# Instructions that consume a transfer, held behind the six traced ahead of them on their engine

## The chip, the cores and the metric

One core of a Trainium2 chip runs the whole program in one launch. The metric is the device time of that core in microseconds (us). Its engines, each with an instruction queue of its own, are TensorE (PE: matmuls and transposes), VectorE (DVE), ScalarE (ACT), GpSimd (POOL) and SyncE (SP, which only issues transfers). Transfers (DMA) run beside them.

## The reference, cut to what matters

One layer of a flow-matching backbone for two groups of tokens: 128 context tokens and 2048 sample tokens of width 1024. Tokens are normed and modulated, one projection makes the columns of three branches, and the branches are merged with sigmoid gates:

```python
proj = jnp.einsum('btd,de->bte', xn, w_in)
qkv, beta, dec, z_a, u_b, v_b, z_b, x_c, z_c, gates = jnp.split(proj, points, axis=-1)
...
o, s_f, s_b = delta_bidir(q, k, v, g, beta, s0_f, s0_b)     # A: chunked gated delta rule, both directions
o_a = rmsnorm(o, o_norm_g) * silu(z_a)
o_b = chunk_sgu(u_b, v_b, sgu_norm_g, w_spatial, b_spatial) * silu(z_b)   # B: gating over chunks of 128
o_c = fourier_mix(x_c, grid) * silu(z_c)                                  # C: Fourier mixing
pb = jnp.einsum('btnw,nwd->btnd', stack(o_a, o_b, o_c), w_branch)
merged = (sigmoid(gates) * pb).sum(over n)
out = jnp.einsum('btd,de->bte', merged, w_out)
```

In branch A each chunk solves a triangular system (which the kernel does with inverses of 32x32 blocks, the "base inverses", and two levels that join them), and a scan carries the state from chunk to chunk.

## The kernel before, in words

**Numbers.** Every float32 operand of a matmul is split into two float16 halves, hi and lo, and a product takes three matmuls (hi·hi, hi·lo, lo·hi; `mm3`, L161 is the line that all of them have). Before it is split an operand is scaled by a power of two that is found from its sum of squares.

**A weight's way** (`converting`, L194 to L223): a weight of 1024x128 (or 512x128 for a branch projection) is loaded into one of two staging buffers `wst` by SP (L204). ACT squares it and sums (L209, into `lo`, which is only scratch at that point: the rows read `wlo<-wst` or `blo<-wst`, each followed by a small read of the accumulator). DVE casts the sum (L175), PE multiplies it with a matrix of ones (`b<-wscb,ones16`), DVE makes the scale from the result (L183 to L187), ACT makes hi (L222, `whi` or `bhi`) and DVE lo (L223). `converting` is a generator, and `weight_step` takes one step of it at each tick of the main loops, so that the next weights are made while PE works with the present ones; `getw` takes the steps that are still missing when a weight is needed. `wnext` counts the weights that were asked for so far.

**The stages.** PE is given the tokens' projections first (branch A's inputs and its chunk matrices, then branch B, then branch C), then three merges, then the output projection. Branch A's scan (`scan`, 34 steps over both directions) runs between the other matmuls: a `Pace` object takes a step of its generator every so many microseconds of main work. A scan step reads `kn` and `v` of a chunk, splits them (`kn16`, L972; `v16`, L907, by `split`), multiplies with the state, joins the levels of the inverse (`level`, L847 to L895, with tiles `ES`, `N`, `Q`, `T`, `R`), and splits `u` and the state S (L907 again, since all of them call `split`). `finish` norms a chunk's output `o` (four squares at L1048 and four products at L1051 on ACT, a transpose on PE at L1055, a product on DVE at L1057 and a square at L1058 on ACT) and stores it.

**Base inverses** (`base_inverse`, five groups): two loads fill `XB`, DVE copies one half transposed (L788), then 31 steps of two DVE operations (L795, L796), two conversions (L801 on ACT, L802 on DVE), and a store to `ei` (L805), from which the levels load `ES` (L847).

**Branch C**: rows of the Fourier transform go through `X` (ACT L1284, DVE L1285 to L1287) between two sets of matmuls.

**Merges** (`merge`, branches 1, 2, 0): for each of eight column blocks `db`, a gate weight `gw` (1024x128) and a branch weight `bw` (512x128); for each of five token blocks 24 matmuls of 512 columns with `gw`, a sigmoid on ACT (L1385, `sg`), 12 matmuls with `bw` on the branch's output `big`, and a product on DVE. `big` is made from `obD` by `branch_block` (a load into one of three buffers `st`, the hi half on ACT at L1355, the lo half on DVE at L1356), for the first merge just ahead of its use, for the others in the last `db` of the merge before.

**Output** (`out_prep`): a row of `merged` is loaded, squared on ACT (L1460), split (L1462 for hi) and multiplied with the output weight `wohi`, `wolo`.

**What sets the order.** The code is traced in program order, and a list scheduler with a timeline model then places the instructions of each engine. It may lift an instruction past others that are traced ahead of it, if its data are ready by its model. Each engine runs its own list strictly in order: an instruction whose transfer has not landed holds back everything behind it.

## Time and profile before

| | |
|---|---|
| time, median of 3 runs | 2198.1 us (2195.02 to 2202.01) |
| the profiled execution's own time | 2200.3 us |
| its span | 2198.2 us |
| instructions | 42667 |
| mean transfer rate | 166 GB/s |
| 1700 to 2000 us: PE busy | 300.0 of 300 us |

The profile is of one execution. In a row in time order the columns are the start and the length in us, the engine, the line, the operation, `out<-in` with the names of the tiles, shapes and count, and in brackets the time that the engine stood idle before the row with what ended it. Matmul lengths overlap: 128x512 matmuls follow each other every 0.216 us though each is shown with 0.35 to 0.38 us. A row of `SPq` is the issue of a transfer. A group's row gives busy time, mean ns of one, and the idle time before its instructions by releaser.

### The profile page before, as it was taken

How to read it: one execution, taken by the hardware profiler on the slowest of the kernel's cores; microseconds unless marked ns; L12 is line 12 of the kernel's file. 1: busy time of each engine (PE TensorE's matmuls, PEld its weight loads, DVE VectorE, ACT ScalarE, POOL GpSimd, SP SyncE). 2: the span in 40 equal slices, each digit the busy share in tenths (PEclk: the TensorE clock that was granted, in tenths of full speed). 3: DMA queues.
4: the chain of work that ended last, by engine and by line, in shares of the span. 5: the costliest groups of instructions: out<-in, count | busy, mean ns of one | idle time of the engine just before them, and what ended most of it. 6: DMA issues, size and time to landing. Idle time of an engine off the chain costs nothing. (4 is left out here: it accounts for less than half of the span.)

```text
span 2198.2 us, 42667 instructions
## 1 busy us (share of the span) xinstructions
PE 2125.9 (97%) x16234; PEld 1213.1 (55%) x16234; DVE 1311.2 (60%) x3140; ACT 1014.4 (46%) x2345; POOL 707.5 (32%) x862
## 2 busy tenths in 40 slices
PE   7999999999999999899899999999999999999998
PEld 3565444455555587777555555555654444444443
DVE  5746745469979698466665555765674544223454
ACT  3644644345466474355544445655553422222332
POOL 1421433223333322432322223344532221222543
PEclk9999999999999999999999999999999999999999
DMA  8324733167777662444655556776664544324542
GB/s 280 141 87 149 260 117 110 61 203 231 241 229 239 198 192 83 126 130 137 203 172 162 164 164 185 240 212 209 200 198 151 168 125 133 118 78 123 174 148 103
DMA packets 304568, 365.09 MB, mean 166 GB/s; under 512 B 39426, under 2 KB 215787, under 8 KB 302315
## 3 DMA queue, kind: packets, MB, share of 16 engines
q1 hardware_dynamic: 289226, 302.19, 45.6%
q0 software_dynamic: 12688, 51.27, 6.4%
q10 hardware_dynamic: 2448, 8.91, 1.0%
q8 instruction: 127, 2.08, 0.4%
q14 instruction: 79, 0.64, 0.1%
HBM read 234.67 MB, written 127.62 MB: 165 GB/s over the span
## 5 line engine op out<-in xcount | busy, mean ns | idle before, releaser
L161 PE MATMUL b<-xh,whi 128*128 128x512 f16 (+1 forms) x1920 | 652.8, 349 | 0.4 <-DVE mrow L1391 0.4
L161 PE MATMUL b<-xl,whi 128*128 128x512 f16 (+1 forms) x1920 | 652.9, 348 | 0.0
L161 PE MATMUL b<-xh,wlo 128*128 128x512 f16 (+1 forms) x1920 | 651.9, 348 | 0.5 <-DVE wlo L223 0.5
L161 PEld LDWEIGHTS <-whi 128*128 128x128 f16 x3904 | 358.8, 98 | 330.0 <-issue 9.4
L161 PEld LDWEIGHTS <-wlo 128*128 128x128 f16 x1952 | 191.7, 98 | 180.8 <-issue 5.0
L161 PE MATMUL b<-big,bhi 128*128 128x512 f16 (+1 forms) x960 | 250.6, 347 | 2.4 <-ACT big L1355 1.9
L1395 POOL TENSOR_TENSOR mrow<-mrow,sg 128x512 f32<-128x512 f32 (+1 forms) x80 | 91.8, 1148 | 293.9 <-DVE sg L1394 225.7
L161 PE MATMUL b<-big,blo 128*128 128x512 f16 (+1 forms) x480 | 162.9, 347 | 0.0
L1385 ACT ACTIVATE sg<-b,winv 128x512 f32<-128x512 f32 (+1 forms) x120 | 74.1, 618 | 174.5 <-PE b L161 173.7
L644 POOL TENSOR_TENSOR cy<-cy,raw 128x545 f32<-128x545 f32 (+1 forms) x48 | 74.9, 1586 | 184.2 <-ACT raw L643 184.2
L161 PEld LDWEIGHTS <-xh 128*128 128x128 f16 x1496 | 117.0, 98 | 28.1
L1394 DVE SCALAR_TENSOR_TENSOR sg<-b,binv,sg 128x512 f32<-128x512 f32 (+1 forms) x80 | 53.4, 667 | 126.1 <-PE b L161 119.3
L161 PEld LDWEIGHTS <-bhi 128*128 128x128 f16 x960 | 86.5, 98 | 73.6 <-issue 2.1
L175 DVE CAST wscb<-wss 128x1 bf16<-128x1 f32 x93 | 14.3, 154 | 148.5 <-ACT wlo L209 67.3
L864 POOL COPY T<-ES 32x256 f16<-32x256 f16 x68 | 30.5, 449 | 202.3 <-DMA ES<-ei 167.1
L161 PE MATMUL b<-whi,xh 128*128 128x128 f16 x544 | 92.9, 219 | 0.0
L161 PE MATMUL b<-wlo,xh 128*128 128x128 f16 x544 | 92.9, 219 | 0.0
L161 PE MATMUL b<-whi,xl 128*128 128x128 f16 x544 | 92.9, 219 | 0.0
L161 PE MATMUL b<-wohi,mh 128*128 128x512 f16 x240 | 90.9, 379 | 1.4 <-ACT mh L1462 1.4
L161 PE MATMUL b<-wohi,ml 128*128 128x512 f16 x240 | 90.8, 379 | 0.3 <-DVE mscb L175 0.3
L161 PE MATMUL b<-wolo,mh 128*128 128x512 f16 x240 | 90.9, 379 | 0.0
L209 ACT ACTIVATE wlo<-wst 128x1024 f16<-128x1024 f32 x52 | 55.0, 1057 | 77.5 <-DMA wst<-in_w_in_dram 74.1
(456 smaller groups left out, 4285.4 us busy)
## 6 DMA issues: line engine op xcount, KB each, us to landing
wst<-in_w_in_dram SPq DMA_DIRECT2D x60, 512.0 KB, 4.9
qkv<-cy POOLq DMA_DIRECT2D x12, 1089.0 KB, 5.4
st<-br SPq DMA_DIRECT2D x48, 256.0 KB, 4.6
mrow<-mrg SPq DMA_DIRECT2D x18, 512.0 KB, 3.6
mrow<-mrg SPq DMA_DIRECT2D x16, 576.0 KB
mrg<-mrow POOLq DMA_DIRECT2D x16, 576.0 KB, 3.6
dc<-dec SPq DMA_DIRECT2D x17, 512.0 KB, 4.7
kq<-qkv SPq DMA_DIRECT2D x34, 256.0 KB, 4.6
```

The costliest lines, as they stand in the source:

```text
L161: PE.matmul(out, l, r, start=start, stop=stop)
L175: V.tensor_copy(sb16, ss)
L209: A.activation(w.lo, st, AF.Square, accum_out=ss)
L644: G.tensor_tensor(y[:, c0:c1], y[:, c0:c1], raw[:, 1 + c0:1 + c1], ALU.mult)
L864: G.tensor_copy(T16[rows(a0, b), :, :, b], ES[0:32, :, 2 * a0 + b, :, wT])
L1385: A.activation(sg, ps, AF.Sigmoid, scale=gw.inv)
L1394: V.scalar_tensor_tensor(sg, ps, binv[:, 1:2], sg, ALU.mult, ALU.mult)
L1395: G.tensor_tensor(mr, mr, sg, ALU.add)
```

## The change

A helper ties an instruction to the six that were traced just ahead of it on the same engine, with a dependency that carries no semaphore: the scheduler may no longer place it ahead of them, and nothing else waits. It is used at six places: the square of a weight, from the seventeenth weight asked for on; DVE's copy that begins a base inverse; the cast of `kn`; the split of `v` in the first step of each scan direction; ACT's half of a branch block; and the square of an output row.

```diff
+    def pinned(made, n=6):
+
+        ins = made.ins
+        before = (i for i in reversed(nc.cur_bb.bb.instructions) if i is not ins and i.engine == ins.engine)
+        for _, i in zip(range(n), before):
+            tc.add_manual_dep(ins, i.name, mybir.DependencyInfo(mybir.DependencyClass.NoSync, mybir.DependencyReason.DATA),
+                              reason="pinned")
+        return made
...
-        A.activation(w.lo, st, AF.Square, accum_out=ss)
+        sq = A.activation(w.lo, st, AF.Square, accum_out=ss)
+        if wnext[0] >= 16:
+            pinned(sq)
...
-        V.tensor_copy(b3(X[64:P, :]), tmp[64:P, :].rearrange("p (i j) -> p j i", j=32))
+        pinned(V.tensor_copy(b3(X[64:P, :]), tmp[64:P, :].rearrange("p (i j) -> p j i", j=32)))
...
-    def split(t_, src, scale=1.0):
-        A.activation(t_[:, 0, :], src, AF.Copy, scale=scale)
+    def split(t_, src, scale=1.0, pin=False):
+        hi = A.activation(t_[:, 0, :], src, AF.Copy, scale=scale)
+        if pin:
+            pinned(hi)
...
-            A.copy(kn16[:, 0, :], kn_)
+            pinned(A.copy(kn16[:, 0, :], kn_))
...
-            split(v16, v_)
+            split(v16, v_, pin=S is None)
...
-            A.activation(o16[:, 0, g, t0:t0 + tn], st, AF.Copy, scale=s)
+            pinned(A.activation(o16[:, 0, g, t0:t0 + tn], st, AF.Copy, scale=s))
...
-            A.activation(ml, mt, AF.Square, accum_out=ss)
+            pinned(A.activation(ml, mt, AF.Square, accum_out=ss))
```

What this does to the lists of the engines is shown at three places. The lines of the changed kernel are 9 to 13 higher: its L218 is L209 (the square), L233 is L222 (hi), L918 is L907 (split), L985 is L972, L1368 is L1355 (a branch block), L1398 is L1385 (sigmoid). The numbers in the names are those of the tiles; they are the same in both kernels.

**ACT at the start of the scan.** `v16_1362` is the first split of `v`; X20 and X21 are tiles of the Fourier rows. Before:

```order
L1284 CAST X20_1140_8304<-b_1309_10337 128x4x65
L1284 CAST X20_1140_8304<-b_1309_10337 128x4x63
L1300 COPY us_1311_10381<-b_1310_10356 128x256
L1328 ACTIVATE yT_1260_9569<-b_1312_10387 128x128
L907 ACTIVATE v16_1362_11064<-sv_1319_10485 128x512
L1284 CAST X21_1141_8305<-b_1313_10395 128x4x65
```

Of the change, where the first level's Q3, T160 and R160 stand ahead of it:

```order
L1282 ACTIVATE xc_1357_10965<-b_1352_10838 128x512
L873 ACTIVATE Q3_1322_10491<-b_1345_10767 32x256
L1262 CAST Y1_1337_10587<-b_1358_10968 128x4x64x2
L233 ACTIVATE whi_1341_10690<-wst_1291_10120,wsc_1350_10831 128x1024
L890 ACTIVATE T160_1321_10489<-b_1353_10887 32x4x32
L890 ACTIVATE R160_1320_10487<-b_1353_10887 32x4x32 x2
L985 CAST kn16_1361_11061<-skn_1318_10483 128x512
L918 ACTIVATE v16_1362_11064<-sv_1319_10485 128x512
```

The split has moved from among the Fourier rows of branch C's third group to those of its last group, behind the cast of `kn`.

**ACT at the start of merge 1.** `big` are the blocks of the branch's output, `sg_1621` is the sigmoid of the second token block, whose 24 matmuls make `b_1613`. Before:

```order
L1355 ACTIVATE big_1569_13392<-st_1584_13430,bsc_1573_13400 128x512
L1385 ACTIVATE sg_1621_13715<-b_1613_13619,winv_1474_12235 128x512
L209 ACTIVATE wlo_1694_14278,wss_1695_14279<-wst_1672_14118 128x1024
L1355 ACTIVATE big_1569_13392<-st_1585_13434,bsc_1573_13400 128x512
L860 ACTIVATE Q3_1322_10491<-b_1654_13944 32x256
L879 ACTIVATE R161_1354_10896<-b_1655_13968 64x4x64
L1355 ACTIVATE big_1569_13392<-st_1586_13438,bsc_1573_13400 128x512
```

Of the change:

```order
L233 ACTIVATE bhi_1574_13405<-wst_1400_11422,wsc_1579_13413 128x512
L1368 ACTIVATE big_1569_13392<-st_1583_13426,bsc_1573_13400 128x512
L873 ACTIVATE Q3_1322_10491<-b_1614_13626 32x256
L1368 ACTIVATE big_1569_13392<-st_1584_13430,bsc_1573_13400 128x512
L1368 ACTIVATE big_1569_13392<-st_1585_13434,bsc_1573_13400 128x512
L1368 ACTIVATE big_1569_13392<-st_1586_13438,bsc_1573_13400 128x512
L1368 ACTIVATE big_1569_13392<-st_1587_13442,bsc_1573_13400 128x512
L1368 ACTIVATE big_1569_13392<-st_1588_13446,bsc_1573_13400 128x512
L1368 ACTIVATE big_1569_13392<-st_1589_13450,bsc_1573_13400 128x512
L1368 ACTIVATE big_1569_13392<-st_1590_13454,bsc_1573_13400 128x512
L985 CAST kn16_1600_13536<-skn_1595_13499 128x512
L1368 ACTIVATE big_1569_13392<-st_1609_13603,bsc_1573_13400 128x512
```

The conversion of the merge's first branch weight now stands directly ahead of the blocks, and nine blocks stand ahead of `sg_1621` (the row after the last one shown), where two stood before.

**ACT and PE at the last branch weight of merge 2, `bhi_2700`.** `sg_2718` is the sigmoid of the last `db`'s first block. ACT before, with the square of that weight in the second row and its conversion in the last but one:

```order
L1058 ACTIVATE of_2636_21959,oss0_479_4088<-o_2623_21817 128x512
L209 ACTIVATE blo_2701_22483,wss_2702_22484<-wst_2681_22303 128x512
L907 ACTIVATE v16_2661_22131<-sv_2646_22040 128x512
L1385 ACTIVATE sg_2665_22173<-b_2657_22082,winv_2609_21699 128x512
L917 ACTIVATE o_2663_22155<-b_2664_22156,eg_239_1394 128x128 x4
L879 ACTIVATE R161_1354_10896<-b_2667_22188 64x4x64
L222 ACTIVATE whi_2668_22205<-wst_2649_22059,wsc_2684_22309 128x1024
L1385 ACTIVATE sg_2679_22286<-b_2671_22209,winv_2609_21699 128x512
L222 ACTIVATE bhi_2700_22482<-wst_2681_22303,wsc_2709_22534 128x512
L209 ACTIVATE wlo_2721_22602,wss_2722_22603<-wst_2706_22528 128x1024
```

ACT of the change:

```order
L1398 ACTIVATE sg_2704_22511<-b_2703_22486,winv_2609_21699 128x128
L1061 ACTIVATE of_2694_22405,oss_2695_22408<-o_2689_22355 128x128 x4
L1064 ACTIVATE o_2689_22355<-o_2689_22355,oss_2695_22408 128x128 x4
L1398 ACTIVATE sg_2718_22584<-b_2717_22559,winv_2685_22314 128x512
L1071 ACTIVATE of_2694_22405,oss0_479_4088<-o_2689_22355 128x512
L218 ACTIVATE blo_2701_22483,wss_2702_22484<-wst_2681_22303 128x512
L233 ACTIVATE bhi_2700_22482<-wst_2681_22303,wsc_2709_22534 128x512
```

PE of the change at the same place, from the last matmul of the gate (`b_2717`) to the first one on `bhi_2700`:

```order
L161 MATMUL b_2717_22559<-xh_4_93,wlo_2669_22206 128x512
L1068 MATMUL b_2696_22425<-cst_1_87,o_2689_22355 128x128 x4
L161 LDWEIGHTS ones16_2_89
L161 MATMUL b_2708_22532<-wscb_2707_22530,ones16_2_89 128x1
L161 MATMUL b_2714_22551<-sg_2571_21394,sel_12_109 2x256 x2
L161 LDWEIGHTS bhi_2700_22482
L161 MATMUL b_2719_22586<-big_1569_13392,bhi_2700_22482 128x512
```

Square, ones-matmul and conversion of that weight have moved from four token blocks ahead of the need to the very place of it, behind the sigmoid and the last square of a chunk's output.

## The prediction

> **What bounds the kernel now.** I read the page first, then the waits of PE, then windows of PE time around those waits, then ACT and DVE in time order inside the windows.
>
> ```profile
> PE 2125.9 (97%) x16234; PEld 1213.1 (55%) x16234; DVE 1311.2 (60%) x3140; ACT 1014.4 (46%) x2345; POOL 707.5 (32%) x862
> 890.00:908.00 18.00, 10.44 (x81) 5.88 (x78) 5.99 (x14) 3.76 (x10) 10.74 (x16) 0.81 0.64 168
> 1056.00:1082.00 26.00, 20.14 (x160) 11.64 (x160) 18.18 (x52) 16.93 (x38) 8.13 (x13) 0.80 0.78 240
> 1100.00:1663.00 563.00, 550.27 (x4956) 328.58 (x4953) 343.43 (x909) 292.84 (x773) 203.35 (x276) 1.00 0.62 189
> 1700.00:2000.00 300.00, 300.00 (x1675) 146.18 (x1674) 109.27 (x296) 83.66 (x135) 62.53 (x64) 1.00 0.37 119
> ```
>
> TensorE (PE) sets the time: it is busy 2125.9 of 2198.2 us, so no change that leaves its work alone can win more than 72 us plus what its clock loses. After each window come its length, then the busy times of PE, weight load, DVE, ACT and POOL, then PE's granted clock. From 890 to 908 PE is idle for 7.6 us and runs at 0.81 of its clock, from 1056 to 1082 it is idle for 5.9 at 0.80, over the 563 us from 1100 to 1663 it is idle for 12.7 us at full clock, and from 1700 to 2000 not at all. So the loss sits in a few places. What ends it there:
>
> ```profile
> 900.28 0.48 PE L161 MATMUL b<-cf,X 128*128 128x128 f16 x3 [7.21 <-DVE X L1286]
> 1061.41 0.26 PE L161 MATMUL b<-S,sk 128*128 128x128 f16 x1 [2.52 <-ACT S L907]
> 1075.78 0.38 PE L161 MATMUL b<-big,bhi 128*128 128x512 f16 x1 [1.60 <-ACT big L1355]
> 1101.50 0.22 PE L161 MATMUL b<-v,R 128*128 128x128 f16 x1 [0.71 <-ACT v L907]
> 1393.35 0.25 PE L161 MATMUL b<-Q,ES 128*128 128x32 f16 x4 [1.77 <-ACT Q L862]
> 1662.47 0.91 PE L1055 MATMUL b<-cst,o 128*128 128x128 f32 x3 [0.90 <-ACT o L1051]
> 2013.11 0.39 PE L161 MATMUL b<-wohi,mh 128*128 128x512 f16 x1 [1.44 <-ACT mh L1462]
> ```
>
> The releasers named are not the culprits; each stood behind an instruction that waited for a transfer. ACT and DVE in time order show it (the bracket is the idle time ahead of the row):
>
> ```profile
> 897.49 0.63 ACT L907 ACTIVATE v<-sv 128x512 f16<-128x512 f32 x1 [6.90 <-DMA sn<-n]
> 898.15 0.69 DVE L908 SCALAR_TENSOR_TENSOR v<-sv,v 128x512 f16<-128x512 f32 x1 [6.49 <-DMA sn<-n]
> 1059.85 0.63 ACT L209 ACTIVATE blo<-wst 128x512 f16<-128x512 f32 x1 [1.42 <-DMA wst<-in_w_branch_dram]
> 1391.14 1.06 ACT L209 ACTIVATE wlo<-wst 128x1024 f16<-128x1024 f32 x1 [4.46 <-DMA wst<-in_w_in_dram]
> 1392.93 0.37 ACT L862 ACTIVATE Q<-b 32x256 f16<-32x256 f32 x1
> ```
>
> At 897.5 both engines had stood 6.5 to 6.9 us at the scan's first split, and the Fourier copies X behind it released PE at 900.28. At 1391 ACT had stood 4.46 us at a weight square; Q, behind it, released PE at 1393.35. Over the run those heads of queue sum to:
>
> ```profile
> ACT wlo L209 <- DMA wst<-in_w_in_dram: 74.1, 26, 7.3
> ACT blo L209 <- DMA wst<-in_w_branch_dram: 31.8, 11, 5.3
> ACT big L1355 <- DMA st<-br: 30.1, 23, 4.2
> ```
>
> That is 136 us of ACT time, but only what PE feels counts.
>
> **What goes.** The change adds no semaphore and no work: it only forbids the scheduler to lift the six kinds of instruction past the six traced ahead on their engine, and the two orders show that it moves them by 20 to 35 us of PE work. (a) Scan start: the 7.21 us gap, and 18 us at 0.81, which is 3.4 us of clock: 10.6. (b) Start of merge 1 (1056 to 1082): gaps of 2.52 and 1.60, and 26 us at 0.80, 5.2 of clock: 9.3. (c) Nine gaps from 1101.50 to 1662.47, each behind a square or a block that waited for its load: 9.7 of that window's 12.7 us. (d) 2013.11, behind four squares of output rows: 1.4. Together 31.0. In the new order a gate weight's square stands over 20 us of PE work after the conversion that frees its staging buffer, far more than a load takes, so those waits do go. The ACT waits from 1700 to 2000 hid behind a PE with no gap, and are worth nothing.
>
> **What comes.** A square that stands later makes its weight later, since cast (L175), the ones-matmul on PE, the scale steps (L183 to L187), the conversion (L222) and only then the first matmul follow. Gate weights keep 20 us. Branch weights, needed one gate gemm later, do not. The rows that price it:
>
> ```profile
> 1551.45 0.63 ACT L209 ACTIVATE blo<-wst 128x512 f16<-128x512 f32 x1 [2.60 <-PE b L1055]
> 1552.21 0.16 DVE L175 CAST wscb<-wss 128x1 bf16<-128x1 f32 x1 [3.03 <-ACT blo L209]
> 1543.84 0.15 DVE L183 COPY wsc<-b 128x1 f32<-128x1 f32 x1
> 1544.28 0.14 DVE L187 TENSOR_SCALAR wsc<-wsc 128x1 int32<-128x1 int32 x1
> 1545.81 0.72 ACT L222 ACTIVATE bhi<-wst,wsc 128x512 f16<-128x512 f32 x1
> 1553.42 0.74 DVE L1057 SCALAR_TENSOR_TENSOR o<-b,pc,of 128x512 f32<-128x512 f32 x1
> 1554.24 0.63 ACT L1058 ACTIVATE of<-o 128x512 f32<-128x512 f32 x1
> 1554.87 0.36 ACT L894 ACTIVATE Q<-b 64x256 f16<-64x256 f32 x1
> ```
>
> Square to the cast's end takes 0.92 (1551.45 to 1552.37), the scale steps 0.58 (1543.84 to 1544.42), the conversion 0.72. (e) The last weight of merge 2, bhi_2700: in the new order its square stands behind `of` (0.63 to the next start), which squares the `o` that DVE makes (0.74) from four transposes, and those stand on PE right after the gate gemm. So, from their end: 0.74, 0.63, 0.92, 0.58 and 0.72, with 0.7 in all for DVE to see the transposes and for the ones-matmul on the way (an estimate, some four to five times a small step of 0.15), make 4.3; PE has 0.3 of other matmuls ahead of the first one on bhi_2700: a gap of 4.0. Before, this conversion stood 28 us ahead. The same sum for the other four that come short: bhi_2216 2.2 (square behind four `o` of the scan), bhi_2473 0.7 (its ones-matmul now right behind the gate gemm, 1.1 us ahead of the need of 1.8), bhi_2556 2.2 (square behind sg, `of`, S and `o`), bhi_2640 1.7 (`of` and v between). Sum 10.8, between 6 (each chain a microsecond shorter, where ACT has caught up) and 18 (below, first rival). A gap above 2.5 us costs clock besides: 2.52 and 1.60 together cost 5.2, 7.21 cost 3.4, so 0 to 3.4 for one; I take 1.7 for the 4.0. (e) is 12.5.
>
> That price of the clock meets the Trainium skill, "TensorE: Matmul & The Clock Gate", Part 1 (The HAM clock gate): the array falls to half rate after an idle window of about 3.4 us, so gaps below that are free. By that rule, if no window falls idle, the 1.7 would be nearly nothing and the sum 1.7 lower; the 0.80 around gaps of 2.52 and 1.60 speaks against it, and I keep the row.
>
> (f) Start of merge 1 in the new order: v, two squares of the Fourier gate, then bhi_1574's square all behind four `o` of the scan; the ones-matmul is 3.5 late and the first block 0.9 more: 4.4, with 1.7 of clock 6.1 in place of 9.3.
>
> (g) Scan start: the copy of the last base inverse (L788) is pinned too and moves 18 us later, among the Fourier row work on DVE.
>
> ```profile
> L802 DVE SCALAR_TENSOR_TENSOR XB<-E,XB 128x1024 f16<-128x1024 f32 x2 | 3.2, 1580 | 1.1 <-ACT XB L801 1.1
> L795 DVE TENSOR_TENSOR XB<-XB,E 128x31 f32<-128x31 f32 (+15 forms) x31 | 11.6, 375 | 0.7
> 884.24 2.88 SPq L805 DMA_DIRECT2D ei<-XB  x2
> 898.36 2.16 SPq L847 DMA_DIRECT2D ES<-ei  x3
> st<-br SPq DMA_DIRECT2D x48, 256.0 KB, 4.6
> ```
>
> Its 31 steps of two (11.6 and about as much) and the two conversions (3.2) now end while X for PE is due on the same DVE queue: X comes some 2 us late. From its store (884.24) to the end of the issue of what reads it (900.5) went 16 us, with a landing like the 4.6 of the branch blocks some 20; in the new order the level's first matmul on ES follows the store by about 15 us of PE work: 0 to 5 late, I take 2.5. (g) is 4.5. The casts of kn (L972) and the copies of the other base inverses have 3 us and more of slack left: nothing, unless a step stalls that is already late. On SP the stores of the base inverses move with their copies; the loads behind them are those of (g).
>
> **The sum.** Minus 10.6, 9.3, 9.7 and 1.4, plus 12.5, 6.1 and 4.5: minus 7.9 us. The profiled execution took 2200.3, so 2192.4; against the median of 2198.1 that is 2190.2, say 2190. A measurement of this kernel tells about 0.3%, 6.6 us, from no change.
>
> **Rivals.** First, slower: the late branch data. It is one mechanism: on ACT, squares and blocks now meet the scan's steps at the end of each gate gemm instead of ahead of it.
>
> ```profile
> 1062.59 0.71 ACT L1355 ACTIVATE big<-st,bsc 128x512 f16<-128x512 f32 x1
> 1069.55 0.72 ACT L1355 ACTIVATE big<-st,bsc 128x512 f16<-128x512 f32 x1 [1.28 <-DMA st<-br]
> ```
>
> At merge 1 nine blocks now stand in a row on ACT ahead of the second block's sigmoid, through three buffers. A round of three takes 0.72, DVE's half (about as much) and 4.6, so 6; the eighth needs two rounds and more, 13 to 15, and PE's order gives it 10: 5 more. At bhi_2216 three blocks stand ahead of u: 1.8. At bhi_2556 S stands behind `of`: 2.1. With 1.7 of clock for three more gaps and 5.2 instead of 1.7 at merge 1, that is 17.5 more: plus 9.6, 2207.7. It decides once the new gaps pass the 31.0 that go. For it: the DMA share of 0.78 from 1056 to 1082; against: before, the second block there waited 7 us after the first and PE felt only 1.60.
>
> Second, no change: the nine gaps of (c) are at S, Q, R, v and `o`, all of the scan's chain; if that chain itself is as late, half of the 9.7 stays: minus 3, 2195.
>
> Third, the full gain: ACT, no longer standing 136 us, catches up, and (e) and (f) fall to 6 and 2: minus 18.5, 2179.6. That the change does nothing is out: the order moved.
>
> **How the numbers follow.** The forecast (minus 4 to minus 14) 0.45, the full gain 0.16, no change 0.14, slower 0.25. Of the forecast's 0.45 about 0.30 lies beyond 6.6 us, so faster is 0.30 + 0.16 = 0.46, the same 0.15 + 0.14 = 0.29, slower 0.25. The range goes from 2174 (the full gain with (g) gone too) to 2210 (the slower rival and 2 us); the forecast's own is 2184 to 2194. Less than 2 in 10 is left out.
>
> **What would show it.** Right: at the scan's start no gap of 7 us and a clock near 1; ACT's waits at L209 and L1355 (as they are numbered before) for transfers well under 136 us; from 1100 to 1663 gaps of PE that end at bhi, blo or the ones-matmul, about 4 us at the last branch weight of merge 2, in place of those at S, Q and `o`. Wrong: such gaps sum to over 25 us with a clock below 1 (the slower rival), or the gaps at S, Q and `o` stay without a transfer behind them (no change). A gap of over 5 us at ES in the scan's start would make (g) wrong.

## The result and the profile after

The changed kernel takes 2225.9 us (median of 6, 2222.8 to 2228.5) against 2200.6 of the kernel before (6, 2195.0 to 2208.6): 1.0115 times as long, 95% interval 1.0098 to 1.0132. The forecast of 2190 was wrong, in sign and outside its range. The profiled execution took 2224.7 us with a span of 2222.7, 24.5 more than before.

ACT's waits for the loads of weights went, as was forecast. By row the sum in us, the number of waits and the longest one:

```profile
ACT big L1368 <- DMA st<-br: 41.3, 25, 3.8
ACT wlo L218 <- DMA wst<-in_w_in_dram: 22.4, 7, 7.2
ACT blo L218 <- DMA wst<-in_w_branch_dram: 3.0, 1, 3.0
```

The squares' 105.9 us of before (74.1 and 31.8) are 25.4. The waits for branch blocks, tied as well, grew from 30.1 to 41.3, so that the 136.0 us of the three rows of before are 66.7. Yet PE's share fell. The page of the changed kernel, and windows of PE time (length, busy times of PE, weight load, DVE, ACT and POOL, clock, DMA share, GB/s):

```profile
PE 2133.8 (96%) x16234; PEld 1222.3 (55%) x16234; DVE 1314.0 (59%) x3140; ACT 1012.8 (46%) x2345; POOL 716.2 (32%) x862
```

```profile
1100.00:1400.00 300.00, 300.00 (x2753) 180.00 (x2752) 172.95 (x470) 140.67 (x351) 83.66 (x132) 1.00 0.58 174
1400.00:1422.00 22.00, 14.02 (x128) 9.07 (x125) 16.97 (x41) 14.81 (x39) 6.96 (x10) 0.76 0.89 278
2030.00:2090.00 60.00, 51.89 (x238) 23.13 (x236) 29.95 (x65) 18.99 (x27) 26.98 (x21) 0.94 0.51 166
```

The same windows of the kernel before:

```profile
1100.00:1400.00 300.00, 293.59 (x2654) 174.82 (x2652) 173.59 (x466) 145.28 (x354) 81.30 (x126) 1.00 0.59 175
1400.00:1422.00 22.00, 19.89 (x201) 12.68 (x200) 15.58 (x43) 14.88 (x41) 8.32 (x14) 1.00 0.86 268
2030.00:2090.00 60.00, 60.00 (x283) 27.28 (x282) 27.62 (x54) 18.16 (x28) 35.21 (x28) 1.00 0.54 180
```

From 1100 to 1400 PE now has no gap at all, where it stood 6.4 us. But at the start of merge 2 (1400 to 1422) it stands 8.0 us instead of 2.1 and its clock falls from 1.00 to 0.76, and among the output rows (2030 to 2090) it stands 8.1 us where it stood none. PE in time order names the new gaps (the brackets):

```profile
888.51 2.26 PE L161 MATMUL b<-cf,X 128*128 128x128 f16 x24 [1.99 <-DVE X L1300]
...
921.92 0.19 PE L161 MATMUL b<-ES,N 128*128 128x32 f16 x1 [5.54 <-DMA N<-n]
...
1062.25 0.22 PE L161 MATMUL b<-v,R 128*128 128x128 f16 x1 [2.31 <-ACT v L918]
...
1413.62 0.27 PE L161 MATMUL b<-u,kn 128*128 128x128 f16 x1 [3.55 <-ACT u L918]
1416.40 1.33 PE L161 MATMUL b<-u,kn 128*128 128x128 f16 x11 [2.27 <-DVE u L921]
...
1602.06 0.22 PE L161 MATMUL b<-S,sk 128*128 128x128 f16 x1 [2.52 <-ACT S L918]
...
1694.16 0.16 PE L161 MATMUL b<-wscb,ones 128*128 128x1 bf16 x1 [3.34 <-DVE wscb L184]
...
2059.27 0.59 PE L161 MATMUL b<-wohi,mh 128*128 128x512 f16 x1 [5.64 <-DVE hh L1533]
2074.39 0.38 PE L161 MATMUL b<-wohi,whi 128*128 128x512 f16 x1 [1.79 <-DVE hh L1533]
```

For a whole account, idle time and slow clock together, I took from the trace for every matmul the distance to the next one's start, less the distance that its shape keeps in gapless work (0.216 us for 128x512, 0.056 for 128x128 in f16 and so on), and summed this over stages of equal PE work. Edges are given by the times of the kernel before. One execution of each kernel was profiled, and a single stage can differ by 2 to 3 us where nothing was changed: merge 1 from 1108 to 1305 loses 2.5 in the kernel before and 0.6 in one_bw (below), whose only tie stands far behind it.

| stage | before | after | change | forecast |
|---|---|---|---|---|
| 0 to 405 | 16.0 | 15.3 | -0.7 | 0 |
| base inverses, 405 to 845 | 24.7 | 20.0 | -4.7 | 0 |
| scan start, 845 to 1017 | 12.6 | 16.5 | +3.9 | -6.1 |
| merge 1 start, 1017 to 1108 | 15.1 | 15.8 | +0.7 | -3.2 |
| merge 1, 1108 to 1305 | 2.5 | -0.2 | -2.7 | } |
| merge 2 start, 1305 to 1431 | 5.7 | 12.3 | +6.6 | } |
| merge 2, 1431 to 1565 | 4.0 | 4.7 | +0.7 | } +2.8 |
| merge 2, 1565 to 1679 | 4.2 | 9.4 | +5.2 | } |
| end of merge 2, 1679 to 1789 | 0.2 | 5.9 | +5.7 | } |
| merge 0, 1789 to 1990 | 0.6 | 0.3 | -0.3 | 0 |
| output, 1990 to 2132 | 1.9 | 11.1 | +9.2 | -1.4 |

The sum of lost time goes from 87.5 to 111.1: 23.6 of the 24.5 us that the span is longer. Three stretches missed their forecast by 10 us and more: the scan's start, the merges (together +15.5 instead of +2.8), and the output rows.

**The start of merge 2.** ACT of the changed kernel ahead of the 3.55 us gap:

```profile
1405.90 0.72 ACT L1368 ACTIVATE big<-st,bsc 128x512 f16<-128x512 f32 x1 [1.35 <-DMA st<-br]
...
1408.70 0.65 ACT L218 ACTIVATE blo<-wst 128x512 f16<-128x512 f32 x1
...
1409.31 1.34 ACT L1368 ACTIVATE big<-st,bsc 128x512 f16<-128x512 f32 x2
1412.34 0.72 ACT L1368 ACTIVATE big<-st,bsc 128x512 f16<-128x512 f32 x1 [1.68 <-DMA st<-br]
1412.96 0.61 ACT L918 ACTIVATE u<-sv 128x512 f16<-128x512 f32 x1
...
1417.01 0.71 ACT L233 ACTIVATE bhi<-wst,wsc 128x512 f16<-128x512 f32 x1
```

From 1408.70 on, one branch square and three blocks stand ahead of `u` at 1412.96, the last of which waits 1.68 us for its load. PE waits for `u` (3.55), and for its lo half, which queues on DVE behind the same blocks' lo halves (2.27).

**The output rows.** The gap at 2059.27 is not about a row's square. `hh` is a product with `gt`, which POOL makes from `gb`, the broadcast of the gate row. Its load, and the conversion ahead of it, before:

```profile
2023.06 1.15 ACT L1462 ACTIVATE whi<-mrow,msc 128x1024 f16<-128x1024 f32 x1 [0.47 <-DVE msc L186]
2025.66 0.33 SPq L1501 DMA_DIRECT2D gb<-gate  x1
```

After:

```profile
2049.28 1.15 ACT L1475 ACTIVATE whi<-mrow,msc 128x1024 f16<-128x1024 f32 x1 [5.39 <-DVE msc L195]
2051.87 0.33 SPq L1514 DMA_DIRECT2D gb<-gate  x1
2056.60 3.75 POOL L1498 TENSOR_TENSOR gt<-gb,inv 128x1024 f32<-128x1024 f32 x2 [20.62 <-DMA gb<-gate]
```

`gb` lives in a pool that is opened where the merge's pool was closed (`ms_.close()`, then `pool(ctx, "op", 2)`), and the last user of the old memory is the split of the row that was loaded into the merge's `mrow`. In both kernels `gb` is issued 2.6 us after that row's hi half starts (2025.66 less 2023.06, 2051.87 less 2049.28), that is when DVE's lo half is done. Ordered behind their forerunners, the squares of the rows now alternate with the conversions of the rows ahead, each of which waits 5 to 7 us for its scale, so that row comes 26 us later (some 15 of them brought along from the stages ahead), and `gb` with it. That `gb` lies in just that row's memory is read from the program and from the equal distance of 2.6 us; the addresses were not looked at.

### The profile page after: what moved, and what is told of

Same layout as the page of the kernel before. It is cut to its first block, busy times and chain, and to the rows that moved or that the text cites. A ratio compares the mean times of both kernels' runs of the same rounds, so it can differ in the third digit from the quotient of the medians.

```text
span 2222.7 us, 42595 instructions
## 1 busy us (share of the span) xinstructions
PE 2133.8 (96%) x16234; PEld 1222.3 (55%) x16234; DVE 1314.0 (59%) x3140; ACT 1012.8 (46%) x2345; POOL 716.2 (32%) x862
## 4 chain that ended last, share of the span: by engine, by line
PE 50%; DMA 4%; DVE 4%; ACT 2%; issue 1%; POOL 1%; SPq 0%; DVEq 0%; POOLq 0%; ACTq 0%
PE b L161 50%; DMA ES<-ei 1%; DMA of<-sz 1%; DMA st<-br 1%; DVE E L807 0%; DMA ei<-XB 0%; DVE XB L806 0%; DMA br<-st 0%; DMA sk<-kT 0%; DVE sv L992 0%; PE b L1068 0%; DVE o L937 0%; DMA mrg<-mrow 0%; POOL st L1150 0%; POOL gt L1498 0%
## 5 line engine op out<-in xcount | busy, mean ns | idle before, releaser
L161 PEld LDWEIGHTS <-whi 128*128 128x128 f16 x3904 | 359.9, 98 | 338.0 <-issue 12.6
L1398 ACT ACTIVATE sg<-b,winv 128x512 f32<-128x512 f32 (+1 forms) x120 | 74.5, 621 | 195.9 <-PE b L161 195.0
L234 DVE SCALAR_TENSOR_TENSOR wlo<-wst,wsc,whi 128x1024 f16<-128x1024 f32 x52 | 71.6, 1379 | 36.8 <-ACT whi L233 36.4
L986 POOL TENSOR_TENSOR kn<-skn,kn 128x512 f16<-128x512 f32 x34 | 40.6, 1194 | 140.9 <-ACT kn L985 129.1
```

The costliest lines, as they stand in the source:

```text
L161: PE.matmul(out, l, r, start=start, stop=stop)
L234: V.scalar_tensor_tensor(w.lo, st, s, w.hi, ALU.mult, ALU.subtract)
L986: G.tensor_tensor(kn16[:, 1, :], kn_, kn16[:, 0, :], ALU.subtract)
L1398: A.activation(sg, ps, AF.Sigmoid, scale=gw.inv)
```

## Experiments

The theory was that the loss has three places with three causes: branch weight squares that now stand at the place of need, output squares that hold back `gb`, and the last base inverse that holds back the scan's first loads. The rivals were that the branch blocks (the data, not the weights) make the loss in the merges, and that late gate squares do. The letters in the texts on record name the theories of their batch. Their "last branch weight of merge 2", as in the prediction and ahead of it, is wrongly named: `bhi_2700` belongs to the last but one of the eight column blocks.

| kernel | time, us | against before (95% interval) |
|---|---|---|
| after | 2225.9 | 1.0115 (1.0098 to 1.0132) |
| no_out | 2214.5 | 1.0083 (1.0062 to 1.0104) |
| no_base | 2231.4 | 1.0161 (1.0146 to 1.0177) |
| no_blocks | 2220.9 | 1.0115 (1.0097 to 1.0133) |
| no_bw | 2209.1 | 1.0056 (1.0037 to 1.0075) |
| only_bw | 2225.1 | 1.0105 (1.0069 to 1.0141) |
| only_gate | 2210.2 | 1.0048 (1.0031 to 1.0065) |
| no_bw_out | 2200.9 | 1.0011 (0.9996 to 1.0026) |
| no_bw_out_bl | 2199.3 | 1.0002 (0.9989 to 1.0015) |
| early_steps | 2216.6 | 1.0083 (1.0065 to 1.0102) |
| early_no_out | 2207.9 | 1.0049 (1.0033 to 1.0065) |
| only_base | 2197.5 | 1.0007 (0.9997 to 1.0017) |
| only_v | 2192.6 | 0.9975 (0.9964 to 0.9985) |
| v_base4 | 2198.4 | 1.0001 (0.9991 to 1.0011) |
| one_bw | 2199.9 | 1.0011 (1.0001 to 1.0021) |
| v_gate_late | 2188.9 | 0.9960 (0.9947 to 0.9972) |

The `no_` and `early_` kernels are edits of the changed kernel, the others of the kernel before with the helper `pinned` added. Each was timed beside the kernel before, whose median lay between 2196.1 and 2200.6 us, so the ratios are what is to be compared.

### One tie undone

**no_out** frees the output squares.

```diff
-            pinned(A.activation(ml, mt, AF.Square, accum_out=ss))
+            A.activation(ml, mt, AF.Square, accum_out=ss)
```

> The changed kernel with the pin on the squares of output rows taken out again. Theory A (each pin has its own stage and its own price): the changed kernel's gap of 5.6 us at 2059, where the output rows' product waits for the gate row gb, whose buffer is part of the merge's memory and comes free only when the pinned, late output rows are split, goes, and with it the 1.8 us gap behind it and some 2 us of half clock; a gap of about 1.4 us at the first output row comes back. Time about 2217 us (8 less than the changed kernel's 2225.9), ratio to the kernel before about 1.0075; the stages before 2000 us unchanged. Theory B (the weight squares' new place on ACT is behind all of it, the other pins are small): under 3 us less, ratio 1.010 to 1.0115.

It is 7 us faster than the change (1.0083 against 1.0115; the intervals just overlap). The lost time of the output stage goes from 11.1 to 4.1, which is 7 us as well, and the 5.64 us gap is gone. The trace shows how: `gb` is issued 2.59 us after the same conversion starts, as in the other two kernels, and that now starts earlier.

```profile
2034.00 1.15 ACT L1475 ACTIVATE whi<-mrow,msc 128x1024 f16<-128x1024 f32 x1 [0.47 <-DVE msc L195]
...
2036.59 0.33 SPq L1514 DMA_DIRECT2D gb<-gate  x1
```

**no_base** frees DVE's copy that begins a base inverse.

```diff
-        pinned(V.tensor_copy(b3(X[64:P, :]), tmp[64:P, :].rearrange("p (i j) -> p j i", j=32)))
+        V.tensor_copy(b3(X[64:P, :]), tmp[64:P, :].rearrange("p (i j) -> p j i", j=32))
```

> The changed kernel with the pin on the copy that starts a base inverse taken out again; the pin on the scan's first split stays. Theory A: the last base inverse ends earlier again, so the gap of 5.5 us at the level's first matmul (its loads come behind the late base inverse's store) and the one of 2.0 us at X go, and the 7.2 us gap of the kernel before does not come back, since its cause was the split: about 7 us less than the changed kernel, 2219 us, ratio about 1.008. Theory B: the scan's start is late because of the order of all of it, under 3 us less.

This went the other way: 1.0161, 10 us slower than the change. The stage of the base inverses loses 26.9 instead of 20.0, so the tie is a gain there, which no theory had foreseen. Two stages of merge 2 lose 8 us more as well (10.1 and 12.1 instead of 4.7 and 9.4), and the next one 4.5 less (1.4 instead of 5.9), though this tie has no instruction there; why, was not settled.

**no_blocks** frees ACT's half of a branch block.

```diff
-            pinned(A.activation(o16[:, 0, g, t0:t0 + tn], st, AF.Copy, scale=s))
+            A.activation(o16[:, 0, g, t0:t0 + tn], st, AF.Copy, scale=s)
```

> The changed kernel with the pin on the branch blocks taken out again. Theory A: at the start of merge 2 the blocks no longer stand ahead of u with a transfer outstanding, so the gaps of 3.6, 2.3 and 1.5 us around 1414 go, with some 4 us of half clock there: about 10 us less than the changed kernel, 2216 us, ratio about 1.007; the start of merge 1 within 3 us of what it was. Theory B: the blocks only follow the late squares, and u stays late behind something else: under 3 us less.

1.0115, as the change: the blocks' own tie is worth nothing on balance, within some 5 us. The start of merge 2 and the stage behind it lose 5.6 us less (10.2 and 1.2), the stage from 1565 2.6 more and the one from 1679 1.1 more. The rival that the blocks' tie makes the loss falls; that the blocks' loads have a part in it is not ruled out by this.

**no_bw** frees the squares of branch weights alone.

```diff
-        if wnext[0] >= 16:
+        if wnext[0] >= 16 and tag != "b":
```

> The changed kernel with the pin on the squares of branch weights taken out again (the gate weights' squares stay pinned). Theory A: the late branch weights (gaps of 2.5 us at 1602 and 3.3 us at 1694 with their half clock) go, and a few of the waits of ACT for a branch weight's load come back, which cost PE 2 to 4 us: 3 to 6 us less than the changed kernel, about 2221 us, ratio about 1.009. Theory B: most of the loss of 25 us goes, 15 us or more, ratio below 1.005, since the branch weights' squares stand behind all of it.

1.0056: 13 us of the 25 are gone by this line, between what the two theories said. From 1108 to 1789 the lost time falls from 32.1 to some 15, at the start of merge 2 from 12.3 to 3.0, though the blocks are still tied there.

### One tie alone

**only_bw** and **only_gate** tie only squares of branch weights, or only those of all the others, from the seventeenth on.

```diff
+        if wnext[0] >= 16 and tag == "b":
+            pinned(sq)
```

```diff
+        if wnext[0] >= 16 and tag != "b":
+            pinned(sq)
```

> The kernel before with one pin alone: on the squares of branch weights. Theory A2 (the branch weights' squares are the largest single cause, by coming late at the two merge starts and in merge 2): slower than before by 10 to 16 us, ratio about 1.006, with PE gaps at the start of merge 2 and at its last branch weights, and no gap of 5 us at the output rows. Rival B2 (they hurt only together with the pinned gate weights and blocks, which fill ACT at the same place): under 4 us slower, ratio below 1.002.

> The kernel before with one pin alone: on the squares of gate weights (and the column weights of branch C, all that come after the sixteenth but branch weights). Theory A2: most of the gaps of the kernel before between 1100 and 1663 us (9.7 us) go, since more than half of them stood behind such a square, and nothing comes late, because these weights keep 20 us of slack: 4 to 8 us faster, ratio about 0.997. Rival B2: ACT's waits for the branch weights and blocks take their place: within 3 us of before.

The branch squares alone cost 1.0105, as much as the whole change and more than the 10 to 16 us expected. From 1108 to 1789 the profiled execution, the slowest of four and 4.6 us above their median, loses 40.8 us instead of 16.6. PE of only_bw at three of its new gaps:

```profile
1403.53 0.22 PE L161 MATMUL b<-u,kn 128*128 128x128 f16 x1 [1.51 <-ACT u L918]
...
1424.57 1.44 PE L161 MATMUL b<-u,sqk 128*128 128x128 f16 x12 [3.08 <-ACT o L930]
...
1706.82 0.16 PE L161 MATMUL b<-wscb,ones 128*128 128x1 bf16 x1 [2.94 <-DVE wscb L184]
```

Most of its gaps end at steps of the scan (`u`, `o`, `v`, Q) on ACT or DVE, one at the weight itself. What stood ahead of the first two on ACT:

```profile
1402.24 0.72 ACT L1368 ACTIVATE big<-st,bsc 128x512 f16<-128x512 f32 x1 [1.55 <-DMA st<-br]
1402.87 0.61 ACT L918 ACTIVATE u<-sv 128x512 f16<-128x512 f32 x1
...
1423.38 1.14 ACT L930 ACTIVATE o<-b,eg 128x128 f32<-128x128 f32 x4 [3.44 <-DMA br<-o]
```

It is no branch square. `u` stands behind a block that waited for its load, and `o` had to wait 3.44 us for an earlier store; the branch square nearest to them, at 1424.39, comes after both. So the time shows what these squares cost, and the trace shows where PE pays for it, but the way from the one to the other was not found. Gate squares were not free either, as I had taken them (4 to 8 us faster was expected): 1.0048. They win 6.9 us from 1108 to 1679 outside merge 2's start (lost time 0.1, 1.6 and 2.1 instead of 2.5, 4.0 and 4.2), and lose 3.3 at the base inverses, 4.9 at the scan's start, 2.1 at merge 1's start and 5.6 in merge 0, where PE waited nowhere before:

```profile
1802.59 0.38 PE L161 MATMUL b<-xh,whi 128*128 128x512 f16 x1 [2.17 <-DVE sg L1407]
```

**only_v** and **only_base** tie only the scan's first split, or only the base copies.

```diff
-            split(v16, v_)
+            split(v16, v_, pin=S is None)
```

```diff
-        V.tensor_copy(b3(X[64:P, :]), tmp[64:P, :].rearrange("p (i j) -> p j i", j=32))
+        pinned(V.tensor_copy(b3(X[64:P, :]), tmp[64:P, :].rearrange("p (i j) -> p j i", j=32)))
```

> The kernel before with one pin alone, on the first split of v in each direction. The forecast's step (a): the 7.2 us gap at the scan's start and its half clock go, and nothing else comes, since the base inverse stays where it was: 7 to 10 us faster, ratio about 0.996. Rival D: the first level's loads (ES, N) come as late as the split did, PE waits there instead, and half or less of it is gained: 0 to 4 us faster, ratio 0.998 to 1.0.

> The kernel before with one pin alone, on the copy that starts a base inverse. The changed kernel without this pin was slower than with it by some 5 us, against the forecast's term (g). Theory C (the copy, waiting for its load at the head of DVE, cost the stages of the base inverses 400 to 790 us some 6 us, which the pin gives back): 4 to 7 us faster than before, ratio about 0.9975, less lost from 400 to 600 and 700 to 790 us of PE's work. Rival D (the gain was there only among the other pins): within 3 us of before.

only_v is faster, 0.9975: 5.5 us, and 4.3 less are lost at the scan's start, about half of the 10.6 forecast for that gap. DVE of only_v shows why:

```profile
891.16 0.42 DVE L1296 TENSOR_TENSOR X<-b,X 128x252 f16<-128x252 f32 x1
898.62 0.49 DVE L1035 TENSOR_SCALAR S<-S,usc 128x512 f32<-128x512 f32 x1 [7.04 <-DMA sqk<-qk]
899.02 0.29 DVE L1298 TENSOR_SCALAR X<-X 128x504 f16<-128x504 f16 x1
```

With `v` out of the way, the scaling of the state S stands at the head of DVE's queue for a load, 7.04 us, and X behind it. PE's gap shrinks from 7.21 to 2.90 and stays. only_base makes no difference (1.0007) out of two large parts: 8.9 us won at the base inverses (24.7 to 15.8), 7.1 lost at the scan's start (12.6 to 19.7). SP and PE of only_base:

```profile
898.02 2.90 SPq L814 DMA_DIRECT2D ei<-XB  x2
...
907.25 0.34 SPq L957 DMA_DIRECT2D skn<-kv  x1
...
913.19 0.83 SPq L856 DMA_DIRECT2D ES<-ei  x2
```

```profile
865.22 1.14 PE L161 MATMUL b<-cf,xc 128*128 128x128 f16 x9 [4.32 <-DVE xc L1281]
...
920.82 0.19 PE L161 MATMUL b<-ES,N 128*128 128x32 f16 x1 [5.99 <-DMA N<-n]
```

The store `ei` of the last inverse stands on SP ahead of the scan's loads: before, it was issued at 884.24 and `skn` at 892.66; here they come 14 us later, and PE's first matmul on ES has no load in time. This is the changed kernel's gap of 5.54.

### Do the parts add up?

**no_bw_out** takes the two edits of no_bw and no_out, **no_bw_out_bl** that of no_blocks besides.

> The changed kernel without two pins, branch weights' squares and output rows' squares. Theory A2: the two savings add, 13 to 17 us and 7 to 11 us off the 25 that were lost: 2198 us where the kernel before has 2197, ratio 0.999 to 1.003. Rival B2: they don't add, since the order behind each is made anew: ratio 1.005 or more.

> As the kernel without the pins on branch weights and output rows, and without the pin on branch blocks too: what is left are the pins on gate weights, base inverses, the cast of kn and the scan's first split. Theory A2: the gaps of 3.3 us at the first blocks of merge 1 and of 3.2 us in merge 0, that PE took in the kernel without the branch weights' pins behind a block whose transfer had not landed, go: 5 us less than with the blocks pinned, ratio about 0.997, faster than both. Rival B2: the blocks' waits come back ahead of the scan's steps: the same or slower than with them pinned.

1.0011 and 1.0002. The two savings of 0.0059 and 0.0032 would make 1.0024 of 1.0115; measured is the same within its interval. Branch squares and output squares thus make nearly the whole 25 us against the kernel before; the gains and losses of all else that the change ties come to about nothing. The 5 us that freeing the blocks was expected to win besides are not there. The cast of `kn` was not tried alone.

That the rest comes to nothing is itself a miss, since it was forecast to win. In no_bw_out the gate squares' waits are as short as in the changed kernel (19.8 us instead of 74.1), but the blocks wait longer than ever:

```profile
ACT big L1368 <- DMA st<-br: 43.9, 27, 4.8
```

From 1108 to 1789 it loses some 16 us, as the kernel before: the gaps behind gate squares are gone, and others have come, such as 2.54 us at S (1420.48), which stood on ACT behind a block that had waited 4.54.

### The tie or the place?

**early_steps** keeps all six ties, but asks for a weight's next step after each half of a merge's column block too, so a branch square is *traced* earlier, and the same tie lets it stand earlier. **early_no_out** also frees the output squares.

```diff
                 (SY if first else G).dma_start(mD[db][:, h0:h0 + hn], mrow)
+                weight_step()
```

> The changed kernel with all its pins, and one weight step more after each half of a merge's column block, so that a branch weight's square and conversion are traced, and with the pin stand, a token block or two earlier; the work is the same. In its order the conversions of the branch weights of merges 1 and 2 stand 4 to 18 us of PE work ahead of their first matmul (1 to 6, four of them behind it, in the changed kernel), but for the first of merge 1 and the last of merge 2, which stay late. Theory A3 (what a pinned branch weight costs is its own lateness and what queues around it): the loss at the start of merge 2 and at its later weights goes as without that pin, 8 to 14 us less than the changed kernel, about 2214 us, ratio 1.005 to 1.008, with the gap at the last weight of merge 2 still there. Rival B3 (it is not the lateness, but the pinned square's place among the blocks at the merge's start): less than 4 us gained, ratio above 1.0095.

> The kernel with the earlier weight steps, without the pin on output rows. Theory A3: 7 to 9 us less than with that pin, as the two don't meet: about 2206 us, ratio 1.001 to 1.005. Rival B3: ratio above 1.006.

1.0083 and 1.0049: with the tie in place some 7 us come back, in both pairs (1.0115 to 1.0083, and 1.0083 to 1.0049 without the output squares), of the branch squares' 13. From 1305 to 1679 the lost time falls from 26.4 to 14.3, though the profiled execution (2223.2 us) is the slowest of four. At one weight of the last but one column block it rises (1679 to 1789: 12.3 instead of 5.9), since its square still stands behind the last square of a chunk's output, which is late there:

```profile
1686.86 0.63 ACT L1071 ACTIVATE of<-o 128x512 f32<-128x512 f32 x1 [1.41 <-DVE o L1070]
...
1687.49 0.61 ACT L218 ACTIVATE blo<-wst 128x512 f16<-128x512 f32 x1
...
1689.21 0.72 ACT L233 ACTIVATE bhi<-wst,wsc 128x512 f16<-128x512 f32 x1 [1.01 <-DVE wsc L195]
```

So about half of the cost lies in the place that the tie gives and not in the tie as such. The edit moves steps of gate weights as well, so how much of it is the branch squares' is not separated.

### The price of one late weight

**one_bw** ties a single square to its place, that of `bhi_2700`.

```diff
+        if tag == "b" and len(wdone) == 66:
+            pinned(sq)
```

> The kernel before with a single instruction pinned: the square of the branch weight bhi_2700, the one for which the forecast worked out a gap of 4.0 us and 1.7 us of clock. Its order differs from before only around that place. Theory A4 (a late branch weight costs by itself what the chain of rows says): a gap of 3 to 4.5 us at its ones-matmul and conversion, some 2 us of half clock, 4 to 7 us slower than before, ratio 1.002 to 1.003. Rival B4 (a late weight alone is cheap, and the changed kernel's losses come from many things late at once): within 2 us of before, ratio below 1.001.

1.0011 (1.0001 to 1.0021), +2.5 us. PE, and its window from 1660 to 1700 (before, 39.10 us were busy there at a clock of 1.00):

```profile
1676.54 0.16 PE L161 MATMUL b<-wscb,ones 128*128 128x1 bf16 x1 [3.35 <-DVE wscb L184]
```

```profile
1660.00:1700.00 40.00, 36.65 (x213) 17.92 (x211) 16.64 (x55) 13.40 (x34) 7.74 (x8) 0.96 0.45 139
```

A gap of 3.35 and 0.04 of 40 us, 1.6, of clock: the forecast for this one weight was 4.0 and 1.7. At its own place the unit price was right. The whole kernel is slower by half of that, 2.5 us (0.2 to 4.6), and by less than the 4 to 7 expected; other stages lose less in the profiled execution, merge 1 among them, where nothing is tied.

### Ties only where there is slack

**v_base4** ties the first split and the base copies but for the last group's, to keep what only_base won and not what it lost.

```diff
+        cp_ = V.tensor_copy(b3(X[64:P, :]), tmp[64:P, :].rearrange("p (i j) -> p j i", j=32))
+        if g < 4:
+            pinned(cp_)
```

> The kernel before with the pin on the scan's first split and the pin on the copies of the base inverses of the first four groups; the last group's copy is left free. Theory C2 (the base pins give back some 9 us between 400 and 790 us, and cost 7 us at the scan's start only through the last group, whose store the first level's loads wait for): both gains add, 10 to 15 us faster than before, ratio 0.993 to 0.996, faster than the kernel with the split's pin alone (0.9975). Rival D2 (freeing the last copy makes it meet the earlier ones, or the first level comes late anyway): 0.9965 or above, no better than the split's pin alone within the intervals.

This brought nothing: 1.0001. The inverses share one buffer XB, so the last copy is late behind the others even when it is free: the store of the group ahead is issued at 843.27 (before 809.71), the load of the last group at 854.49 (before 838.42). DVE of v_base4:

```profile
859.85 1.03 DVE L797 COPY XB<-XB 64x1024 f32<-64x1024 f32 x1 [10.00 <-DMA XB<-nd]
```

It starts where it does in the changed kernel (859.5), 14 us later than in the kernel before (845.3). The win is kept (16.4 instead of 24.7) and so is the loss (20.1 instead of 12.6).

**v_gate_late** ties the first split and, of the squares, only the gate weights from merge 1's second to merge 2's last.

```diff
+        if tag == "w" and 38 < len(wdone) < 68:
+            pinned(sq)
```

> The kernel before with the pin on the scan's first split and on the squares of the merges' gate weights only (from the second of merge 1 to the last of merge 2); branch weights, blocks, base inverses, the cast of kn and output rows are free. In its order the gate weights keep 20 us and more between conversion and use, the branch weights 3 us and more. Theory E (the forecast's step (c) is to be had alone: the gaps of the kernel before in the merges go with the gate squares' waits, and nothing comes late): 4 to 8 us faster than with the split's pin alone, ratio to before 0.994 to 0.996. Rival F (a branch weight's square now stands right behind its gate weight's and waits for its own load there, so ACT stands as long, and PE with it): no better than the split's pin alone, ratio 0.997 or above.

0.9960 (0.9947 to 0.9972), 8.7 us faster than before. Against only_v (0.9975, 0.9964 to 0.9985) 3 us are won, where 4 to 8 were expected, and the intervals overlap: by time alone the gain over only_v is likely, not shown. ACT's waits for these loads, and the windows behind 1100 (before, 293.59 busy of 300 and, from 1400 to 1663, 256.68 of 263):

```profile
ACT wlo L218 <- DMA wst<-in_w_in_dram: 31.7, 11, 7.2
...
ACT blo L218 <- DMA wst<-in_w_branch_dram: 20.4, 6, 5.0
```

```profile
1100.00:1400.00 300.00, 295.00 (x2650) 175.16 (x2650) 174.47 (x464) 145.51 (x355) 81.27 (x128) 1.00 0.59 178
1400.00:1663.00 263.00, 260.78 (x2345) 157.61 (x2346) 170.19 (x444) 148.50 (x424) 123.07 (x146) 1.00 0.67 205
```

Idle time from 1100 to 1663 goes from 12.7 to 7.2 us. From 1431 to 1679 the kernel loses 2.2 instead of 8.2; only_v, without these ties, loses 9.0 there. Part of the gaps of (c) is thus to be had, without a single late branch weight.

## Why the prediction was wrong

**Two groups of terms.** no_bw_out parts the sum in two. What it leaves tied was forecast to win 15.8: minus 10.6 (a), minus 9.7 (c), plus 4.5 (g). Measured is a loss of 2.4 (1.0011). Branch and output squares, which it frees, were forecast to cost 7.9: plus 12.5 (e), plus 6.1 (f), minus 9.3 (b), whose longer gap stood behind a branch square, and minus 1.4 (d). Measured is 22.9, the rest of the 25.3 us by which the change is slower. So 18 us of the miss are gains that did not come, and 15 are costs put too low. The split is not exact, since the two groups act on each other: in no_bw_out the freed branch squares wait again, 23.2 us in all.

**(a), the scan's start: right in kind, half its size.** The wait at `v` went, but 10.6 was counted as if nothing else were late there. Alone it gave 4.3 in its stage and 5.5 in time (only_v), since the scaling of S stands for the same batch of loads, on DVE, ahead of the same X. What is late next was not asked for this gap. The 10.6 was too much as a sum besides. A low clock costs nothing while PE stands, and of the 6.83 us at half clock (896.92 to 903.75) PE was busy in 3.47: 1.7 of clock and not 3.4, so 8.9 in all.

**(g), the base inverse: too low, and one-sided.** 4.5 was forecast; only_base lost 7.1 at the scan's start. The 0 to 5 us for ES reckoned from the store to ES alone; but the scan's loads stand on SP behind that store, and they came later with it (the store by 13.8 us, `skn` by 14.6). The 5.54 us gap there is the one that the text named as making (g) wrong. The other side was missed: "copies of the other base inverses: nothing" hid a gain of 7 to 9 us in their stage (only_base, no_base). Both together with (a) make the scan's start +3.9 and the inverses -4.7, -0.8 in place of -6.1.

**(b) and (f), merge 1: near.** +0.7 against -3.2; the longest gap is at v (2.31), not at the ones-matmul or the first block. The nine blocks ahead of the second sigmoid, 5 us in the rival, cost nothing that shows as a gap there.

**(c): gaps exchanged for others.** The gaps at S, Q and `o` behind gate squares went. From 1108 to 1305 the loss went to nothing, but it is as low in one_bw (0.6), whose only tie stands far behind, and in only_v (0.3), which ties no weight, so the tie of the squares has not been shown to have done it. In merge 2 new gaps stand in their place, with the branch squares free as well (no_bw_out); only_gate and v_gate_late, with blocks and branch squares free, keep part of the gain (3.7 and 2.2 from 1431 to 1679 instead of 8.2). So the step that failed here is that a gap which ends behind one waiting step was booked as won, while blocks with loads of their own stood behind it on the same queue: their waits rose from 30.1 to 41.3 us.

**(e) and the first rival: the sum over late weights failed.** (e) priced each late weight by its own chain, square to conversion, and summed to 12.5; the rival added 1.8 for three blocks ahead of `u`. The price of a single chain was right at its place (one_bw 3.35 and 1.6; in the changed kernel 3.34 at 1694). The sum over them was not: five late weights were priced at 12.5, and in these stages the branch squares lose 24.2 more when they are tied alone (only_bw, 40.8 against 16.6, in an execution above its median) and some 17 among the other ties (32.1 against some 15 in no_bw). The chains were priced one by one, each up to its own first matmul. The gaps of only_bw stand mostly elsewhere, at steps of the scan, and this second bill was left out. The way by which a late square makes those steps late stays open: the two rows shown have no square ahead of them, but a block and a store that were waited for. How the cost divides among the weights was measured for `bhi_2700` alone.

The first rival had places right (u, S, a clock below 1: 3.55, 2.27 and 2.52, 0.76 over 22 us), and the sign. But 6.8 us of its price were for blocks, and the blocks' tie is not the cause: freed, they change the time by nothing and merge 2's start from 12.3 to 10.2, while freeing the squares makes it 3.0 and tying the squares alone 15.2. Blocks stand ahead of `u` in both traces, tied or not; why their loads came late there was not settled. The rival's 17.5 was too little. The text's mark for it, gaps of over 25 us in the merges, was too high besides: the idle time from 1100 to 1700 is 20.2 us, and the rest is clock.

**(d), the output squares: wrong sign.** -1.4 was read from the gap that goes. What the square releases was not followed: it delays the row's conversion, that the freeing of the merge's memory, that `gb`, `gt` and `hh`: 5.64 and 1.79 us, 7 us by no_out. In the trace of before POOL already waited 8.7 us for `gb`, and `gt` followed at once; the prediction left that row out.

The misses: merges 12.7, output 10.6, scan start 10.0, merge 1 3.9, against them -4.7 at the inverses, -0.7 ahead of them and -0.3 in merge 0: 31.5 of the 32.4 by which the span's change (24.5) missed the sum (-7.9).

**The price of the clock** was kept from the row and not from the Trainium skill, "TensorE: Matmul & The Clock Gate", Part 1, whose idle window of about 3.4 us would leave shorter gaps free. The window around the gap of 2.52 of the changed kernel bears the row out:

```profile
1596.00:1616.00 20.00, 15.89 (x144) 9.96 (x143) 8.67 (x30) 11.47 (x35) 7.20 (x10) 0.91 0.66 209
```

That is 0.09 of 20 us, 1.8, of clock (1.5 of it while PE was busy) beside 4.1 us of idle time, no gap of it above 2.52. The half clock stands from 1602.44 to 1605.85, just behind that gap.

## What to carry to other kernels

An order-only tie takes a wait from the head of a queue and pays with the moved step's place: price it by the slack of everything behind it, its consumers' chain and whatever its last read sets free (a buffer, a pool's memory, a store ahead of loads in the same queue), not by the waits that it ends. Ask of each gap that is to go what waits next behind it on the same queue, since that often takes its place. The price of one late step, right where it was measured alone, did not add up: five priced at 12.5 cost 17 to 24, most of it at other steps than their own. Tie only steps with slack to spare: two of the six kinds, cut to where they have it, won 8.7 us (5.5 of them by the scan's first split alone), and all six lost 25.

## What was not expected of the hardware

The granted clock falls behind gaps as short as 2.5 us, and each time it stays at half for about the same stretch or a multiple of it. In windows of the traces it is 0.50 for 3.41 us behind the gap of 3.35 in one_bw (1676.64 to 1680.05) and behind that of 2.52 above, for 6.83 us within and behind the one of 7.21 before (896.92 to 903.75), and for 13.6 us at merge 2's start of the changed kernel (1411.3 to 1424.9). It costs half of what PE is busy in that stretch: 1.7, 1.5, 1.7 and 3.8 us. Two gaps of 1.77 and 1.80 before (1391 to 1404) left it at 1.00. And a wait that an engine shows says little of what TensorE feels: in the same three rows ACT's waits for transfers fell from 136.0 to 66.7 us while the kernel became 25 us slower.
